# Batched matrix product on one core: groups of four matrices with longer transfer runs, in place of groups of two

## Chip, cores, metric

One core of a Trainium2 chip (trn2) runs the kernel. The time is device microseconds of one execution, given as a median of several runs. The experiments ran on two chips, and each is compared with the kernel before in the same rounds.

## The reference

```python
b1, b2, m, k, n = 8, 16, 256, 512, 384
def reference(x, weight):            # x [8,16,256,512], weight [8,16,512,384], float32
    return np.matmul(x, weight).astype(np.float32)
```

That is 128 independent products. x has 67 MB, weight 101 MB, out 50 MB: 218 MB must cross between HBM (the large memory) and SBUF (the core's own memory; PSUM, below, is where PE leaves its results).

## The kernel before

Five engines run their own programs and meet at semaphores. SP issues all transfers on one queue; DVE casts x and weight to bf16 and copies the transposed x out of PSUM; PE transposes and multiplies; ACT copies the products into the store buffer. G is 2 matrices a group. A partition holds R = 4 consecutive rows of the group, so an x run is 4 x 512 x 4 B = 8 KB, an out run 6 KB, and a weight run (4 rows of one matrix) 6 KB. A *run* is one contiguous piece; each run moves as one transfer packet (the records have packets of 8192 and 6144 B, and one of 4 B for each engine and transfer). The code is cut, and comments in it are added.

```python
    G = 2; C = P // G; R = G * M // P; J = R // G; NG = B // G
    AHEAD = 4
    XS, WS, OS = AHEAD, AHEAD * G, 8          # slots for x, weight, out
    ...
    def load(e, n, n0):
        wait(e, x_cast, n - XS + 1)
        e.dma_start(x_sb[n0 % XS][:],
            x_rows[bass.ds(n * (G * M), G * M)].rearrange("(p r) k -> p r k", r=R),
        ).then_inc(x_in[n0 % XS], 16)
        for i in range(G):                    # one weight transfer a matrix
            wait(e, w_cast, n * G + (i + 1 - WS))
            e.dma_start(w_sb[(n0 * G + i) % WS][:], ...).then_inc(w_in[(n0 * G + i) % WS], 16)
    ...
    @block.sync                               # SP: the order of the queue
    def _(e):
        U = OS
        for n in range(AHEAD):
            load(e, n, n)
        rounds = (NG - AHEAD) // U
        with e.Fori(0, rounds) as t:
            for s in range(U):
                load(e, t * U + (AHEAD + s), AHEAD + s)
                store(e, t * U + s, s)
        for n in range(rounds * U, NG):
            if n + AHEAD < NG:
                load(e, n + AHEAD, n + AHEAD)
            store(e, n, n)
        ...
```

Of the kernel before, what the change touches and what calls it, by code (L numbers as in the profile page):

```python
# [10 lines left out]
@with_exitstack  # L11
def kernel(
    ctx: ExitStack,
    tc: tile.TileContext,
    x: bass.AP,
    weight: bass.AP,
    out: bass.AP,
):
    nc = tc.nc
    P = 128  # L20

    b1, b2, M, K = x.shape
    _, _, _, N = weight.shape
    B = b1 * b2
    KO = K // P

    x_rows = x.rearrange("b1 b2 m k -> (b1 b2 m) k")
    w_rows = weight.rearrange("b1 b2 k n -> (b1 b2 k) n")
    o_rows = out.rearrange("b1 b2 m n -> (b1 b2 m) n")

    fp32 = mybir.dt.float32
    bf16 = mybir.dt.bfloat16



    G = 2
    C = P // G
    R = G * M // P
    J = R // G
    NG = B // G  # L40

    AHEAD = 4

    XS, WS, OS = AHEAD, AHEAD * G, 8
    BS, TS, WBS = 2, 2, 4
    PT, PO = 4, 2

    ctx.enter_context(tc.tile_critical())  # L48

    def sbuf(name, shape, dtype, n):  # L50
        return [
            ctx.enter_context(nc.sbuf_tensor(f"{name}{s}", shape, dtype)) for s in range(n)
        ]

    def psum(name, shape, dtype, n):
        return [
            ctx.enter_context(nc.psum_tensor(f"{name}{s}", shape, dtype)) for s in range(n)
        ]

    def sems(name, n):  # L60
        return [tc.alloc_semaphore(f"{name}{s}") for s in range(n)]


    identity = sbuf("identity", [P, P], fp32, 1)[0]
    x_sb = sbuf("x_sb", [P, R, K], fp32, XS)
    x_bf = sbuf("x_bf", [P, R, K], bf16, BS)


    x_t = sbuf("x_t", [P, J, KO // 2, G, G, C, 2], bf16, TS)
    w_sb = sbuf("w_sb", [P, KO, N], fp32, WS)  # L70
    w_bf = sbuf("w_bf", [P, KO, N], bf16, WBS)
    out_sb = sbuf("out_sb", [P, R, N], fp32, OS)
    pt = psum("pt", [P, 2, KO // 2, P], fp32, PT)
    po = psum("po", [P, J, 512], fp32, PO)




    x_in, w_in, o_out = sems("x_in", XS), sems("w_in", WS), sems("o_out", OS)
    id_done, x_cast, w_cast, t_copied, t_made, p_made, o_copied = (  # L80
        sems(name, 1)[0]
        for name in (
            "id_done", "x_cast", "w_cast", "t_copied", "t_made", "p_made", "o_copied"
        )
    )
    T = R // 2

    def wait(e, sem, value):
        if not isinstance(value, int) or value > 0:
            e.wait_ge(sem, value)  # L90


    def load(e, n, n0):
        wait(e, x_cast, n - XS + 1)
        e.dma_start(  # L95
            x_sb[n0 % XS][:],
            x_rows[bass.ds(n * (G * M), G * M)].rearrange("(p r) k -> p r k", r=R),
        ).then_inc(x_in[n0 % XS], 16)
        for i in range(G):
            wait(e, w_cast, n * G + (i + 1 - WS))  # L100
            e.dma_start(  # L101
                w_sb[(n0 * G + i) % WS][:],
                w_rows[bass.ds(n * (G * K) + i * K, K)].rearrange(
                    "(p ko) n -> p ko n", ko=KO
                ),
            ).then_inc(w_in[(n0 * G + i) % WS], 16)

    def store(e, n, n0):
        e.wait_ge(o_copied, n * G + G)  # L109
        e.dma_start(  # L110
            out=o_rows[bass.ds(n * (G * M), G * M)].rearrange("(p r) n -> p r n", r=R),
            in_=out_sb[n0 % OS][:],
        ).then_inc(o_out[n0 % OS], 16)

    def cast(e, n, n0, t):

        e.wait_ge(x_in[n0 % XS], t * 16)
        wait(e, t_made, n * T + (1 - BS) * T)
        e.tensor_copy(out=x_bf[n0 % BS][:], in_=x_sb[n0 % XS][:]).then_inc(x_cast, 1)  # L119

        def cast_w(i):
            e.wait_ge(w_in[(n0 * G + i) % WS], t * 16)
            wait(e, p_made, n * G + (i + 1 - WBS))
            e.tensor_copy(  # L124
                out=w_bf[(n0 * G + i) % WBS][:], in_=w_sb[(n0 * G + i) % WS][:]
            ).then_inc(w_cast, 1)

        cast_w(0)
        wait(e, p_made, n * G + (1 - TS) * G)
        for q in range(T):  # L130
            e.wait_ge(t_made, n * T + (q + 1))  # L131
            j, g = divmod(2 * q, G)
            e.tensor_copy(  # L133
                out=x_t[n0 % TS][:, j, :, :, g : g + 2].rearrange(
                    "k h i g c e -> k g (h i) (c e)"
                ),
                in_=pt[(n0 * T + q) % PT][:].bitcast(bf16).rearrange(
                    "k g h (i ce) -> k g (h i) ce", i=G
                ),
            ).then_inc(t_copied, 1)  # L140
        for i in range(1, G):
            cast_w(i)

    def multiply(e, n, n0):
        words = x_bf[n0 % BS][:].bitcast(fp32)
        e.wait_ge(x_cast, n + 1)
        for q in range(T):
            wait(e, t_copied, n * T + (q + 1 - PT))
            for rr in range(2):
                for h in range(KO // 2):  # L150
                    ins = e.transpose(  # L151
                        pt[(n0 * T + q) % PT][:, rr, h, :],
                        words[:, 2 * q + rr, h :: KO // 2],
                        identity[:],
                    )
            ins.then_inc(t_made, 1)
        e.wait_ge(t_copied, n * T + T)
        for i in range(G):
            e.wait_ge(w_cast, n * G + (i + 1))
            wait(e, o_copied, n * G + (i + 1 - PO))  # L160
            for j in range(J):
                for ko in range(KO):
                    ins = e.matmul(  # L163
                        po[(n0 * G + i) % PO][:, j, :N],
                        x_t[n0 % TS][:, j, ko // 2, i, :, :, ko % 2].rearrange(
                            "k g c -> k (g c)"
                        ),
                        w_bf[(n0 * G + i) % WBS][:, ko, :],
                        start=(ko == 0),
                        stop=(ko == KO - 1),  # L170
                    )
            ins.then_inc(p_made, 1)

    def copy_out(e, n, n0, t):

        wait(e, o_out[n0 % OS], t * 16)
        for i in range(G):
            e.wait_ge(p_made, n * G + (i + 1))
            for g in range(G):
                ins = e.copy(  # L180
                    out=out_sb[n0 % OS][i * C : (i + 1) * C, g::G, :],
                    in_=po[(n0 * G + i) % PO][g * C : (g + 1) * C, :, :N],
                )
            ins.then_inc(o_copied, 1)

    block = ctx.enter_context(nc.Block())

    @block.gpsimd
    def _(e):
        e.memset(identity[:], 0.0).then_inc(id_done, 1)  # L190
        e.wait_ge(id_done, 1)
        make_identity(nc, identity[:], nomemset=True)
        e.drain().then_inc(id_done, 1)

    @block.sync
    def _(e):
        U = OS
        for n in range(AHEAD):
            load(e, n, n)
        rounds = (NG - AHEAD) // U  # L200
        with e.Fori(0, rounds) as t:  # L201
            for s in range(U):
                load(e, t * U + (AHEAD + s), AHEAD + s)
                store(e, t * U + s, s)
        for n in range(rounds * U, NG):
            if n + AHEAD < NG:
                load(e, n + AHEAD, n + AHEAD)
            store(e, n, n)
        for s in range(OS):
            e.wait_ge(o_out[s], 16 * (NG // OS))  # L210

    @block.vector
    def _(e):
        U = XS
        for n in range(U):
            cast(e, n, n, 1)
        with e.Fori(1, NG // U) as t:
            for s in range(U):
                cast(e, t * U + s, s, t + 1)

    @block.tensor
    def _(e):
        U = 4
        e.wait_ge(id_done, 2)
        for n in range(U):
            multiply(e, n, n)
        with e.Fori(1, NG // U) as t:
            for s in range(U):
                multiply(e, t * U + s, s)

    @block.scalar
    def _(e):
        U = OS
        for n in range(U):
            copy_out(e, n, n, 0)
        with e.Fori(1, NG // U) as t:
            for s in range(U):
                copy_out(e, t * U + s, s, t)


# [28 lines left out]
```

## Time and profile before

| | before |
|---|---|
| median time of the first three runs | 524.96 us |
| the run that was profiled | 526.41 us, span 524.6 us |
| moved, mean rate over the span | 218.16 MB, 416 GB/s |
| busy: PE, DVE, ACT | 65%, 52%, 39% |
| transfer queue | 99.9% |

No compute engine is near full, and the transfer engines are full except at both ends. The prediction below shows and reads the lines. One thing to notice here already: the profiled run was 1.45 us slower than the median that the prediction starts from.

### The profile page before, as it was taken

What the parts mean: (1) busy time and instruction counts of PE and PEld (TensorE: products, weight loads), DVE (VectorE), ACT (ScalarE), POOL (GpSimd) and SP (SyncE); (2) the same over time, 40 slices, a digit from 0 to 9 for tenths busy, and PEclk for the clock granted to TensorE, in tenths of its full rate; (3) what the DMA queues carried; (4) which work ended last, traced back from release to release, by engine and by line L of the source; (5) the groups of instructions that cost most, each with busy time, mean ns of one, the idle gap of its engine ahead of it and who ended that gap; (6) DMA issues with size and microseconds to landing.
All of it is one profiled execution on the core that took longest, in us unless ns stands there. A gap on an engine that the chain in (4) does not pass through costs nothing.

```text
span 524.6 us, 5588 instructions
## 1 busy us (share of the span) xinstructions
PE 338.9 (65%) x1536; PEld 191.9 (37%) x1536; DVE 272.4 (52%) x320; ACT 204.3 (39%) x257; POOL 0.7 (0%) x6
## 2 busy tenths in 40 slices
PE   3755676756747576675776656666657666766764
PEld 2533333333333343343333333333334333433331
DVE  4655454464554554645545446455454464554641
ACT  1652424344333343342433434444334334344242
POOL 0000000000000000000000000000000000000000
PEclk9997868688787877878778778787787878778686
DMA  8999999999999999999999999999999999999995
GB/s 335 421 415 414 422 420 424 424 424 421 424 423 423 424 423 424 425 420 425 423 423 424 420 423 426 421 424 425 422 425 422 424 424 422 424 424 422 426 423 238
DMA packets 36868, 218.16 MB, mean 416 GB/s; under 512 B 4096, under 2 KB 4096, under 8 KB 28672
## 3 DMA queue, kind: packets, MB, share of 16 engines
q1 hardware_dynamic: 36864, 218.12, 99.9%
q14 instruction: 3, 0.02, 0.0%
q8 instruction: 1, 0.02, 0.0%
HBM read 167.77 MB, written 50.33 MB: 416 GB/s over the span
## 4 chain that ended last, share of the span: by engine, by line
SPq 73%; DMA 15%; issue 7%; PE 2%; DVE 1%; ACTq 0%; DVEq 0%; ACT 0%
SPq L101 47%; DMA w_sb<-in_weight_dram 15%; SPq L110 14%; SPq L95 10%; PE po L163 2%; SPq L90 1%; DVE x_t L133 1%; DVE w_bf L124 0%; SPq L109 0%; ACTq _compat.py:109 0%; SPq L201 0%; PE pt L151 0%; DVEq L90 0%; DVEq L131 0%; ACT out_sb L180 0%
## 5 line engine op out<-in xcount | busy, mean ns | idle before, releaser
L180 ACT COPY out_sb<-po 64x768 f32<-64x768 f32 x256 | 203.0, 793 | 314.4 <-PE po L163 311.7
L163 PE MATMUL po<-w_bf,x_t 128*128 128x384 bf16 x1024 | 251.9, 419 | 95.3 <-DVE x_t L133 95.3
L163 PEld LDWEIGHTS po<-w_bf,x_t 128*128 128x128 bf16 x1024 | 119.4, 122 | 216.6 <-issue 182.0
L119 DVE CAST x_bf<-x_sb 128x2048 bf16<-128x2048 f32 x64 | 78.5, 1227 | 200.0 <-DMA x_sb<-in_x_dram 200.0
L124 DVE CAST w_bf<-w_sb 128x1536 bf16<-128x1536 f32 x128 | 122.3, 955 | 40.2 <-DMA w_sb<-in_weight_dram 40.2
L151 PE MATMUL pt<-identity,x_bf 128*128 128x128 f32 x512 | 87.7, 322 | 83.8 <-DVE x_bf L119 83.5
L151 PEld LDWEIGHTS pt<-identity,x_bf 128*128 128x128 f32 x512 | 72.5, 211 | 109.1 <-issue 107.9
L133 DVE COPY x_t<-pt 128x1024 bf16<-128x1024 bf16 x128 | 82.2, 683 | 1.1 <-PE pt L151 1.1
L180 ACT ACT_TABLE_LOAD x1 | 1.3, 1283 | 0.9 <-SPq L48 0.9
masks.py:199 POOL TENSOR_SCALAR_AFFINE_SELECT identity<-identity 128x128 f32<-128x128 f32 x1 | 0.3, 293 | 0.2 <-POOL identity L190 0.2
L190 POOL MEMSET identity<- 128x128 f32 x1 | 0.2, 204 | 0.5 <-SPq L48 0.5
L253 POOL MEMSET const-bfloat16-1.0<- 128x1 bf16 x1 | 0.1, 101 | 0.0
L253 POOL MEMSET const-uint8-127<- 128x1 uint8 x1 | 0.1, 101 | 0.0
L253 POOL MEMSET const-float32-0.0<- 128x1 f32 x1 | 0.1, 98 | 0.2 <-issue 0.2
L253 POOL MEMSET const-float32-1.0<- 128x1 f32 x1 | 0.1, 98 | 0.0
## 6 DMA issues: line engine op xcount, KB each, us to landing
w_sb<-in_weight_dram SPq DMA_DIRECT2D x128, 768.0 KB, 22.3
x_sb<-in_x_dram SPq DMA_DIRECT2D x64, 1024.0 KB, 22.6
out_dram<-out_sb SPq DMA_DIRECT2D x64, 768.0 KB, 21.7
```

The lines of the kernel that those rows point to most:

```text
L90: e.wait_ge(sem, value)
L95: e.dma_start(x_sb[n0 % XS][:], x_rows[bass.ds(n * (G * M), G * M)].rearrange("(p r) k -> p r k", r=R),).then_inc(x_in[n0 % XS], 16)
L101: e.dma_start(w_sb[(n0 * G + i) % WS][:], w_rows[bass.ds(n * (G * K) + i * K, K)].rearrange("(p ko) n -> p ko n", ko=KO),).then_inc(w_in[( ...
L110: e.dma_start(out=o_rows[bass.ds(n * (G * M), G * M)].rearrange("(p r) n -> p r n", r=R), in_=out_sb[n0 % OS][:],).then_inc(o_out[n0 % OS] ...
L119: e.tensor_copy(out=x_bf[n0 % BS][:], in_=x_sb[n0 % XS][:]).then_inc(x_cast, 1)
L124: e.tensor_copy(out=w_bf[(n0 * G + i) % WBS][:], in_=w_sb[(n0 * G + i) % WS][:]).then_inc(w_cast, 1)
L133: e.tensor_copy(out=x_t[n0 % TS][:, j, :, :, g : g + 2].rearrange("k h i g c e -> k g (h i) (c e)"), in_=pt[(n0 * T + q) % PT][:].bitcast( ...
L151: ins = e.transpose(pt[(n0 * T + q) % PT][:, rr, h, :], words[:, 2 * q + rr, h :: KO // 2], identity[:],)
L163: ins = e.matmul(po[(n0 * G + i) % PO][:, j, :N], x_t[n0 % TS][:, j, ko // 2, i, :, :, ko % 2].rearrange("k g c -> k (g c)"), w_bf[(n0 * G ...
L180: ins = e.copy(out=out_sb[n0 % OS][i * C : (i + 1) * C, g::G, :], in_=po[(n0 * G + i) % PO][g * C : (g + 1) * C, :, :N],)
L190: e.memset(identity[:], 0.0).then_inc(id_done, 1)
L253: nc = _bacc.Bacc("TRN2", target_bir_lowering=False, num_devices=1)
```

## The change

The intent is fewer and longer runs: groups of four with 16 KB runs of x and 12 KB runs of out, weight as before. The last four matrices are two pairs, so that the last chain of compute stays short. Stores are issued behind the third later group instead of the fourth, but groups are twice as big. Semaphores start with a bias, so that no special first round is needed.

```diff
-    G = 2
-    R = G * M // P
-    AHEAD = 4
-    XS, WS, OS = AHEAD, AHEAD * G, 8
+    Q = 4
+    QUADS = B // Q - 1
+    PAIRS = [(QUADS, QUADS * Q), (QUADS + 1, QUADS * Q + 2)]
+    J = M // P
+    XS, WS, OS = 2, 8, 4
+    LAG = 3
...
+            x_sb[a.slot(XS)][:, : J * G],
+            x_rows[bass.ds(a.m * M, G * M)].rearrange("(p r) k -> p r k", r=J * G),
...
+            out=o_rows[bass.ds(a.m * M, G * M)].rearrange("(p r) n -> p r n", r=J * G),
+            in_=out_sb[a.slot(OS)][:, : J * G],
...
             for g in range(G):            # now four copies of 32 partitions a matrix
                 ins = e.copy(
-                    out=out_sb[n0 % OS][i * C : (i + 1) * C, g::G, :],
+                    out=out_sb[a.slot(OS)][i * C : (i + 1) * C, g : J * G : G, :],
...
+                load(e, At(t, U, LAG + s))
+                store(e, At(t, U, s))
```

More of the change, by code (lines that the diff above doesn't have):

```diff
@@ L32 @@
     bf16 = mybir.dt.bfloat16
-    G = 2
-    C = P // G
-    R = G * M // P
-    J = R // G
-    NG = B // G
-    AHEAD = 4
-    XS, WS, OS = AHEAD, AHEAD * G, 8
+    Q = 4
+    QUADS = B // Q - 1
+    PAIRS = [(QUADS, QUADS * Q), (QUADS + 1, QUADS * Q + 2)]
+    GROUPS = QUADS + 2
+    J = M // P
+    XS, WS, OS = 2, 8, 4
     BS, TS, WBS = 2, 2, 4
     PT, PO = 4, 2
+    LAG = 3
     ctx.enter_context(tc.tile_critical())
@@ L64 @@
     identity = sbuf("identity", [P, P], fp32, 1)[0]
-    x_sb = sbuf("x_sb", [P, R, K], fp32, XS)
-    x_bf = sbuf("x_bf", [P, R, K], bf16, BS)
-    x_t = sbuf("x_t", [P, J, KO // 2, G, G, C, 2], bf16, TS)
+    x_sb = sbuf("x_sb", [P, J * Q, K], fp32, XS)
+    x_bf = sbuf("x_bf", [P, J * Q, K], bf16, BS)
+    x_t = sbuf("x_t", [P, J * KO // 2 * Q * P * 2], bf16, TS)
     w_sb = sbuf("w_sb", [P, KO, N], fp32, WS)
     w_bf = sbuf("w_bf", [P, KO, N], bf16, WBS)
-    out_sb = sbuf("out_sb", [P, R, N], fp32, OS)
+    out_sb = sbuf("out_sb", [P, J * Q, N], fp32, OS)
     pt = psum("pt", [P, 2, KO // 2, P], fp32, PT)
     po = psum("po", [P, J, 512], fp32, PO)
-    x_in, w_in, o_out = sems("x_in", XS), sems("w_in", WS), sems("o_out", OS)
     id_done, x_cast, w_cast, t_copied, t_made, p_made, o_copied = (
@@ L85, with __init__, slot, turn @@
     )
-    T = R // 2
-    def wait(e, sem, value):
-        if not isinstance(value, int) or value > 0:
-            e.wait_ge(sem, value)
-    def load(e, n, n0):
-        wait(e, x_cast, n - XS + 1)
+    x_in, w_in, o_out = sems("x_in", XS), sems("w_in", WS), sems("o_out", OS)
+    BIAS = 8
+    class At:
+        def __init__(self, t, U, s, G=Q, m=None):
+            self.t, self.U, self.s, self.G = t, U, s, G
+            self.n = t * U + s
+            self.m = self.n * Q if m is None else m
+            self.m0 = s * Q if m is None else m
+            self.old = self.m - (Q if s <= QUADS else 2)
+        def slot(self, S):
+            return self.s % S
+        def turn(self, S):
+            if isinstance(self.t, int):
+                return self.n // S
+            assert self.U % S == 0
+            return self.t * (self.U // S) + self.s // S
+        def w_turn(self, i):
+            if isinstance(self.t, int):
+                return (self.m + i) // WS
+            assert self.U * Q % WS == 0
+            return self.t * (self.U * Q // WS) + (self.s * Q + i) // WS
@@ L95, in load @@
+    def load(e, a):
+        G = a.G
+        if not isinstance(a.n, int) or a.n >= XS:
+            e.wait_ge(x_cast, a.n - XS + 1)
         e.dma_start(
-            x_sb[n0 % XS][:],
-            x_rows[bass.ds(n * (G * M), G * M)].rearrange("(p r) k -> p r k", r=R),
-        ).then_inc(x_in[n0 % XS], 16)
+            x_sb[a.slot(XS)][:, : J * G],
+            x_rows[bass.ds(a.m * M, G * M)].rearrange("(p r) k -> p r k", r=J * G),
+        ).then_inc(x_in[a.slot(XS)], 16)
         for i in range(G):
-            wait(e, w_cast, n * G + (i + 1 - WS))
+            if not isinstance(a.m, int) or a.m + i >= WS:
+                e.wait_ge(w_cast, a.m + (i + 1 - WS))
@@ L101, in load @@
             e.dma_start(
-                w_sb[(n0 * G + i) % WS][:],
-                w_rows[bass.ds(n * (G * K) + i * K, K)].rearrange(
-                    "(p ko) n -> p ko n", ko=KO
-                ),
-            ).then_inc(w_in[(n0 * G + i) % WS], 16)
-    def store(e, n, n0):
-        e.wait_ge(o_copied, n * G + G)
-        e.dma_start(
-            out=o_rows[bass.ds(n * (G * M), G * M)].rearrange("(p r) n -> p r n", r=R),
-            in_=out_sb[n0 % OS][:],
-        ).then_inc(o_out[n0 % OS], 16)
@@ L115, in cast, with store @@
-    def cast(e, n, n0, t):
-        e.wait_ge(x_in[n0 % XS], t * 16)
-        wait(e, t_made, n * T + (1 - BS) * T)
-        e.tensor_copy(out=x_bf[n0 % BS][:], in_=x_sb[n0 % XS][:]).then_inc(x_cast, 1)
+                w_sb[(a.m0 + i) % WS][:],
+                w_rows[bass.ds(a.m * K + i * K, K)].rearrange("(p ko) n -> p ko n", ko=KO),
+            ).then_inc(w_in[(a.m0 + i) % WS], 16)
+    def store(e, a):
+        G = a.G
+        e.wait_ge(o_copied, a.m + (G + BIAS))
+        e.dma_start(
+            out=o_rows[bass.ds(a.m * M, G * M)].rearrange("(p r) n -> p r n", r=J * G),
+            in_=out_sb[a.slot(OS)][:, : J * G],
+        ).then_inc(o_out[a.slot(OS)], 16)
@@ L121, in cast_w, with xt_view, cast @@
+    def xt_view(a):
+        return x_t[a.slot(TS)][:, : J * KO // 2 * a.G * P * 2].rearrange(
+            "k (j h i g c e) -> k j h i g c e", j=J, h=KO // 2, i=a.G, g=a.G, e=2
+        )
+    def cast(e, a):
+        G = a.G
         def cast_w(i):
-            e.wait_ge(w_in[(n0 * G + i) % WS], t * 16)
-            wait(e, p_made, n * G + (i + 1 - WBS))
+            e.wait_ge(w_in[(a.m0 + i) % WS], a.w_turn(i) * 16 + 16)
+            e.wait_ge(p_made, a.m + (i + 1 - WBS + BIAS))
             e.tensor_copy(
-                out=w_bf[(n0 * G + i) % WBS][:], in_=w_sb[(n0 * G + i) % WS][:]
+                out=w_bf[(a.m0 + i) % WBS][:], in_=w_sb[(a.m0 + i) % WS][:]
@@ L126, in cast_w @@
             ).then_inc(w_cast, 1)
+        e.wait_ge(x_in[a.slot(XS)], a.turn(XS) * 16 + 16)
+        e.wait_ge(t_made, a.old + BIAS)
+        e.tensor_copy(
+            out=x_bf[a.slot(BS)][:, : J * G], in_=x_sb[a.slot(XS)][:, : J * G]
+        ).then_inc(x_cast, 1)
         cast_w(0)
-        wait(e, p_made, n * G + (1 - TS) * G)
-        for q in range(T):
-            e.wait_ge(t_made, n * T + (q + 1))
+        e.wait_ge(p_made, a.old + BIAS)
+        xt = xt_view(a)
+        for q in range(G):
+            e.wait_ge(t_made, a.m + (q + 1 + BIAS))
@@ L132, in cast @@
             j, g = divmod(2 * q, G)
             e.tensor_copy(
-                out=x_t[n0 % TS][:, j, :, :, g : g + 2].rearrange(
-                    "k h i g c e -> k g (h i) (c e)"
-                ),
-                in_=pt[(n0 * T + q) % PT][:].bitcast(bf16).rearrange(
+                out=xt[:, j, :, :, g : g + 2].rearrange("k h i g c e -> k g (h i) (c e)"),
+                in_=pt[(a.m0 + q) % PT][:].bitcast(bf16).rearrange(
                     "k g h (i ce) -> k g (h i) ce", i=G
@@ L142, in cast, with multiply @@
             cast_w(i)
-    def multiply(e, n, n0):
-        words = x_bf[n0 % BS][:].bitcast(fp32)
-        e.wait_ge(x_cast, n + 1)
-        for q in range(T):
-            wait(e, t_copied, n * T + (q + 1 - PT))
+    def multiply(e, a):
+        G = a.G
+        words = x_bf[a.slot(BS)][:].bitcast(fp32)
+        e.wait_ge(x_cast, a.n + 1)
+        for q in range(G):
+            e.wait_ge(t_copied, a.m + (q + 1 - PT + BIAS))
             for rr in range(2):
@@ L151, in multiply @@
                     ins = e.transpose(
-                        pt[(n0 * T + q) % PT][:, rr, h, :],
+                        pt[(a.m0 + q) % PT][:, rr, h, :],
                         words[:, 2 * q + rr, h :: KO // 2],
@@ L156, in multiply @@
             ins.then_inc(t_made, 1)
-        e.wait_ge(t_copied, n * T + T)
+        xt = xt_view(a)
+        e.wait_ge(t_copied, a.m + (G + BIAS))
         for i in range(G):
-            e.wait_ge(w_cast, n * G + (i + 1))
-            wait(e, o_copied, n * G + (i + 1 - PO))
+            e.wait_ge(w_cast, a.m + (i + 1))
+            e.wait_ge(o_copied, a.m + (i + 1 - PO + BIAS))
             for j in range(J):
@@ L163, in multiply @@
                     ins = e.matmul(
-                        po[(n0 * G + i) % PO][:, j, :N],
-                        x_t[n0 % TS][:, j, ko // 2, i, :, :, ko % 2].rearrange(
-                            "k g c -> k (g c)"
-                        ),
-                        w_bf[(n0 * G + i) % WBS][:, ko, :],
+                        po[(a.m0 + i) % PO][:, j, :N],
+                        xt[:, j, ko // 2, i, :, :, ko % 2].rearrange("k g c -> k (g c)"),
+                        w_bf[(a.m0 + i) % WBS][:, ko, :],
                         start=(ko == 0),
@@ L172, in multiply, with copy_out, quad, groups @@
             ins.then_inc(p_made, 1)
-    def copy_out(e, n, n0, t):
-        wait(e, o_out[n0 % OS], t * 16)
+    def copy_out(e, a):
+        G = a.G
+        C = P // G
+        e.wait_ge(o_out[a.slot(OS)], a.turn(OS) * 16 + 16)
         for i in range(G):
-            e.wait_ge(p_made, n * G + (i + 1))
+            e.wait_ge(p_made, a.m + (i + 1 + BIAS))
             for g in range(G):
                 ins = e.copy(
-                    out=out_sb[n0 % OS][i * C : (i + 1) * C, g::G, :],
-                    in_=po[(n0 * G + i) % PO][g * C : (g + 1) * C, :, :N],
+                    out=out_sb[a.slot(OS)][i * C : (i + 1) * C, g : J * G : G, :],
+                    in_=po[(a.m0 + i) % PO][g * C : (g + 1) * C, :, :N],
                 )
             ins.then_inc(o_copied, 1)
+    def quad(n):
+        return At(0, 1, n)
+    pairs = [At(0, 1, n, 2, m) for n, m in PAIRS]
+    def groups(e, U, body):
+        with e.Fori(0, QUADS // U) as t:
+            for s in range(U):
+                body(e, At(t, U, s))
+        for n in range(QUADS // U * U, QUADS):
+            body(e, quad(n))
+        for a in pairs:
+            body(e, a)
     block = ctx.enter_context(nc.Block())
@@ L197, in _ @@
         U = OS
-        for n in range(AHEAD):
-            load(e, n, n)
-        rounds = (NG - AHEAD) // U
+        every = [quad(n) for n in range(QUADS)] + pairs
+        for a in every[:LAG]:
+            load(e, a)
+        rounds = (QUADS - LAG) // U
         with e.Fori(0, rounds) as t:
             for s in range(U):
-                load(e, t * U + (AHEAD + s), AHEAD + s)
-                store(e, t * U + s, s)
-        for n in range(rounds * U, NG):
-            if n + AHEAD < NG:
-                load(e, n + AHEAD, n + AHEAD)
-            store(e, n, n)
+                load(e, At(t, U, LAG + s))
+                store(e, At(t, U, s))
+        for n in range(rounds * U, GROUPS):
+            if n + LAG < GROUPS:
+                load(e, every[n + LAG])
+            store(e, every[n])
         for s in range(OS):
-            e.wait_ge(o_out[s], 16 * (NG // OS))
+            e.wait_ge(o_out[s], 16 + 16 * ((GROUPS - s + OS - 1) // OS))
     @block.vector
     def _(e):
-        U = XS
-        for n in range(U):
-            cast(e, n, n, 1)
-        with e.Fori(1, NG // U) as t:
-            for s in range(U):
-                cast(e, t * U + s, s, t + 1)
+        e.sem_inc(t_copied, BIAS)
+        groups(e, 2, cast)
     @block.tensor
     def _(e):
-        U = 4
+        e.sem_inc(t_made, BIAS)
+        e.sem_inc(p_made, BIAS)
         e.wait_ge(id_done, 2)
-        for n in range(U):
-            multiply(e, n, n)
-        with e.Fori(1, NG // U) as t:
-            for s in range(U):
-                multiply(e, t * U + s, s)
+        groups(e, 2, multiply)
     @block.scalar
     def _(e):
-        U = OS
-        for n in range(U):
-            copy_out(e, n, n, 0)
-        with e.Fori(1, NG // U) as t:
-            for s in range(U):
-                copy_out(e, t * U + s, s, t)
+        e.sem_inc(o_copied, BIAS)
+        for s in range(OS):
+            e.sem_inc(o_out[s], 16)
+        groups(e, OS, copy_out)
 _INS = ['x', 'weight']
```

## The prediction

> **What bounds the kernel now.** I read the page first: busy shares, slices, queue, chain, issues.
>
> ```profile
> PE 338.9 (65%) x1536; PEld 191.9 (37%) x1536; DVE 272.4 (52%) x320; ACT 204.3 (39%) x257; POOL 0.7 (0%) x6
> DMA  8999999999999999999999999999999999999995
> GB/s 335 421 415 414 422 420 424 424 424 421 424 423 423 424 423 424 425 420 425 423 423 424 420 423 426 421 424 425 422 425 422 424 424 422 424 424 422 426 423 238
> q1 hardware_dynamic: 36864, 218.12, 99.9%
> SPq 73%; DMA 15%; issue 7%; PE 2%; DVE 1%; ACTq 0%; DVEq 0%; ACT 0%
> w_sb<-in_weight_dram SPq DMA_DIRECT2D x128, 768.0 KB, 22.3
> x_sb<-in_x_dram SPq DMA_DIRECT2D x64, 1024.0 KB, 22.6
> out_dram<-out_sb SPq DMA_DIRECT2D x64, 768.0 KB, 21.7
> ```
>
> No compute engine passes 65%; the transfer engines are full from the second slice to the last but one. The chain blames the queue of SP, but an issue lands 22 us later: at 424 GB/s some 9 MB stand queued, and SP only waits for room. So the bytes set the time (218.1 MB / 524.6 us = 416 GB/s), and only three things can shorten it: cost per transfer packet, the unfilled start, and the unfilled end. I therefore asked for the stretches, and the waits.
>
> ```profile
> 0.00:13.10 13.10, 5.06 (x18) 3.07 (x19) 5.27 (x6) 1.61 (x2) 0.70 (x6) 1.00 0.84 335
> 200.00:300.00 100.00, 66.54 (x292) 37.10 (x290) 52.31 (x61) 39.30 (x51) 0.00 (x0) 0.78 1.02 423
> 511.00:524.60 13.60, 5.93 (x21) 2.82 (x19) 2.74 (x4) 3.17 (x4) 0.00 (x0) 0.63 0.59 246
> ACT out_sb L180 <- PE po L163: 311.7, 92, 10.6
> PE po L163 <- DVE x_t L133: 95.3, 64, 1.7
> ```
>
> The last three numbers of a stretch are granted clock, DMA share and GB/s. The middle is flat at 423 with a DMA share of 1.02; the last 13.6 us move only 246. ACT waits for PE most of the time, so it has room.
>
> From the packet records of the trace I took medians: a packet of 8192 B (x) takes 309 ns, one of 6144 B (weight and out) 234, and the 4 B packet that ends each transfer 9. That is a straight line: (8192 - 6144)/(309 - 234) = 27.3 B/ns, and 309 - 8192/27.3 = 9 ns fixed. But packets overlap slightly (share 1.02), so I also took the distance between the landings of successive transfers. In the start, where only loads run, x takes 2.482 us and weight 1.881. Over the 8 packets of each engine that is 310 and 235 ns: again 27.3 B/ns and 9 to 10 ns fixed. Stores on their own, at the end, take 1.826 us, 228 ns a packet: only 3 ns fixed. Mixed, one old group of two matrices takes 8.05 us.
>
> **The end.** The timeline shows how it is made.
>
> ```profile
> 510.72 0.96 DVE L124 CAST w_bf<-w_sb 128x1536 bf16<-128x1536 f32 x1 [0.60 <-DMA w_sb<-in_weight_dram]
> 513.10 4.91 PE L163 MATMUL po<-w_bf,x_t 128*128 128x384 bf16 x16 [1.09 <-DVE x_t L133]
> 518.05 1.59 ACT L180 COPY out_sb<-po 64x768 f32<-64x768 f32 x2 [0.57 <-PE po L163]
> 519.67 0.33 SPq L110 DMA_DIRECT2D out_dram<-out_sb  x1
> ```
>
> The last weight lands at 510.2 (mean of the 16 engines; the slowest is 2.3 us later), the last store at 522.8: 12.6 us. Four older stores lie behind that weight and take 4 x 1.83 = 7.3 of them, the last store itself 1.83, so some 3.5 us are empty.
>
> **What the Trainium skill says.** "DMA: Bandwidth & Descriptors", Specifications, gives a fabric ceiling of 435 GB/s; the trace's 27.3 B/ns on 16 engines is 437 without the fixed part, and 423 with it, so it agrees. The same page, "Why small descriptors are slow (HBM only)", names a fixed overhead per packet of about 3 cycles; the trace has one, 9 ns for loads. Its iDMA section lists a load stream of 4 KiB rows alone at 408.7 GB/s; my line, 9 + 4096/27.3 = 159 ns, gives 412, so it also holds below the sizes seen here. "Latency and other measured facts" warns of row pitches of 512 KiB and more at powers of two; the runs here stay contiguous and their pitch goes from 8 to 16 KiB. No run yet shows that size.
>
> **The change, part by part.**
>
> *Longer runs.* Four matrices now need one x transfer of 128 runs of 16 KB instead of two of 8 KB, and one store with 12 KB runs instead of two with 6. Weight stays as it was. Per engine and four matrices: x loses 8 packets of 9 ns and one 4 B packet, 0.08 us; out loses 8 packets of 3 ns and one 4 B packet, 0.03. Against that, turning from store to load seems to save a little (2.482 + 2 x 1.881 + 1.826 = 8.07 against 8.05 measured), and half of those turns vanish: +0.02. Sum -0.09 us a group of four, x31 = -2.8 us. Had stores the same 9 ns, and counting every 4 B packet, it would be (16 x 9 + 2 x 9) x 31 = -5.0 us. I take -3.2.
>
> *The end.* The last four matrices are two pairs, so the last compute chain is the old one: 12.6 us from last weight to last landing. But stores now lag three groups: behind the last weight lie two stores of 1.5 MB and one of 0.75, 3 x 1.83 us plus 2 x 1.83 = 9.1 us, where there were 7.3. One store of 0.75 MB moves from ahead of the last load to behind it, into the empty time: up to -1.8 us. The slowest engine, 2.3 us late, has less emptiness than the mean, so I take -1.4.
>
> *Buffers.* x has 2 x 2 MB instead of 4 x 1 MB, weight 8 slots, out 4 x 1.5 instead of 8 x 0.75 MB: the same bytes. A load of x now waits for the cast of the group two before it. When that cast ends, four weights (3 MB), one x group and its weights and a store, about 9 MB, still stand in the queue, some 20 us. So no gap: 0.
>
> *ACT.* Four copies of 32 partitions for each matrix instead of two of 64. A copy's time goes by its 768 elements a partition (793 ns), so 504 copies x 0.793 = 400 us, 77%. The table load is now listed inside the loop: 7 x 1.28 = 9 us more at most. Still under the 16.0 us of a group: 16 x 0.793 = 12.7.
>
> *Other.* The x cast doubles in size and halves in count; PE's work is equal; counters with a bias remove special first rounds and cost well under 1 us.
>
> Sum: 524.96 - 3.2 - 1.4 = **520.4 us**, -0.9%.
>
> **Rivals.** (1) *Compute becomes the bound.* With two PSUM output buffers, the loop of a group of four is: ACT copies two matrices 6.4 us, PE multiplies the last one 2.4, transposes with their copies by DVE about 3.4 (0.6 + 4 x 0.68), PE multiplies the first 2.4: 14.6 us against 16.0 of transfers. If the x_t copies, whose inner runs halve, rose to 1.1 us, it would be 16.3, and the time about 525 + 31 x 0.2 - 1.4 = 530. For it: ACT at 77% and PE's idle before products, 95 us, tied to x_t. Against: the element count and data width are the same. (2) *Long runs gain nothing or lose*, if a 16 KB run is cut into packets of 8 KB or less: then only the end is left, 523.5; if power-of-two starts collide in memory, x slows: 5% of its 159 us (64 x 2.482) is +8, and the time about 531. Against: 8 KB runs show no such loss beside 6 KB ones. (3) *The end gains nothing*, if ACT and PE, behind on the last group of four, delay the pairs: 521.8. I traced it: the last four are copied some 21.5 us after their x lands, the last pair's weights arrive 27 us after it. (4) *All 9 ns per packet are saved, also on stores, and the whole 1.8 at the end*: 518.
>
> **Range and chances.** Transfers -2.5 to -5.0, the end 0 to -1.8, with some room for rival 1: 517.5 to 523.5. Over 2% faster (514.5) would need 8.7 us from the packets besides the whole 1.8 of the end, against 5.0 at the most; slower by 2% (535.5) needs more than rival 1 or 2 makes of it.
>
> **What would show it.** Packets of 16384 B at about 609 ns and of 12288 B at 453 to 459; data packets fewer by 7,900 out of 32,768. x of four landing 4.88 us after its predecessor, a store of four in about 3.65; groups of four every 16.0 us instead of 16.1; middle slices at 426 GB/s. ACT at 77 to 79% with copies still near 793 ns, and x_t copies near 683. From the last weight to the last landing still 12.6 us, with about 1.7 empty. I am wrong if middle slices drop below 423, if DMA slices in the middle fall below 9, or if 16384 B packets are absent.

## The result, and the profile after

Ratios here are the mean time of one kernel's runs over that of the other's of the same rounds, so not quite the ratio of the medians quoted beside them.

The changed kernel took 524.12 us (median of 4; 523.48 to 524.36) against 525.28 for the kernel before: ratio 0.9972, interval 0.995 to 0.9994. It is faster, but by 1.2 to 1.5 us where 4.6 were predicted, and outside the predicted range.

The page of the kernel after: span, busy shares, transfer slices, packets, queue, the group of ACT's copies, ACT's table loads, and the issues with their time to landing.

```profile
span 521.7 us, 5583 instructions
PE 323.8 (62%) x1536; PEld 192.3 (37%) x1536; DVE 270.0 (52%) x289; ACT 406.9 (78%) x511; POOL 0.7 (0%) x6
DMA  8999999999999999999999999999999999999996
GB/s 330 424 422 423 421 427 423 424 423 423 426 431 424 422 421 426 428 429 421 420 427 427 428 424 421 423 427 429 427 422 421 425 429 428 422 423 423 426 427 258
q1 hardware_dynamic: 27936, 218.12, 99.8%
L213 ACT COPY out_sb<-po 32x768 f32<-32x768 f32 (+1 forms) x504 | 397.9, 790 | 107.4 <-PE po L197 100.6
L213 ACT ACT_TABLE_LOAD x7 | 9.0, 1283 | 1.6 <-ACTq L277 1.5
x_sb<-in_x_dram SPq DMA_DIRECT2D x31, 2048.0 KB, 29.6
```

Much of what was predicted is there: ACT at 78% with copies of 790 ns and seven table loads, 27,936 packets instead of 36,864, and a flat transfer row. The packet records show 16384 B packets at 611 ns in the median and 12288 B at 460, within 2 ns of what was worked out. The stretches of 100 us in the middle move 425 and 424 GB/s where they moved 423 and 424:

```profile
200.00:300.00 100.00, 66.18 (x291) 38.63 (x289) 51.05 (x55) 78.48 (x100) 0.00 (x0) 0.73 1.01 425
300.00:400.00 100.00, 61.48 (x296) 36.10 (x296) 50.56 (x54) 82.86 (x105) 0.00 (x0) 0.80 1.01 424
```

The prediction expected 426. The end (timeline; cast of the second last weight, last products, last copies, issue of the last store) has the same length as before, 8.8 us from the first of these lines to the last against 8.95:

```profile
507.13 0.96 DVE L152 CAST w_bf<-w_sb 128x1536 bf16<-128x1536 f32 x1 [0.60 <-DMA w_sb<-in_weight_dram]
509.34 4.95 PE L197 MATMUL po<-w_bf,x_t 128*128 128x384 bf16 x16 [0.97 <-DVE x_t L167]
514.33 1.59 ACT L213 COPY out_sb<-po 64x768 f32<-64x768 f32 x2 [0.56 <-PE po L197]
515.95 0.33 SPq L136 DMA_DIRECT2D out_dram<-out_sb  x1
```

**The place to look is the spread of the 16 engines.** Each transfer raises its semaphore 16 times, and the trace keeps the time of each. I take it as once for each engine: a transfer has 144 packets (36,864 for 256 transfers), 16 times 8 of data and one of 4 B. The kernel waits for all 16, so a transfer counts as landed when the last has come. Sorted for one weight transfer near 480 us of a second trace of the changed kernel, the last engine is 3.6 us behind the median one and the last but one 1.3. In the first trace of before it is 2.3 against 1.0, in its second 2.4 against 1.5. From about 260 us on, in the changed kernel's second trace from 100 us on, the last one falls behind alone, and steadily: behind the median one it is 1.6 and 2.2 us late at 250 us and 2.8 and 3.5 at 450 in the two traces of the changed kernel, 1.4 and 1.55 and then 2.3 and 2.4 before. That it is one and the same engine is likely from this, but the records do not name it.

So I took two speeds for four matrices: the mean of all engines (packet records, between 20 and 200 MB) and the slowest (a straight line through the last landing of each weight, 17th to 120th of 128). The third number is how far the last landing of the last weight is behind the mean of its 16.

| kernel | mean, us | slowest, us | behind at the last weight, us |
|---|---|---|---|
| before, two traces | 16.110, 16.100 | 16.156, 16.135 | 2.30, 2.27 |
| after, two traces | 16.057, 16.064 | 16.093, 16.129 | 2.77, 3.35 |
| both_short | 16.136 | 16.204 | 3.57 |
| store_short | 16.076 | 16.133 | 3.17 |
| short_spread | 16.035 | 16.103 | 3.23 |
| before_batched | 16.131 | 16.238 | 4.27 |
| before_later1 | 16.099 | 16.146 | 2.48 |
| after_lag4 | 16.053 | 16.126 | 3.41 |
| long_spread | 16.021 | 16.097 | 3.25 |
| long_quarters_lag4 | 16.003 | 16.109 | 4.26 |
| act_stores | 16.028 | 16.096 | 2.84 |
| before_act | 16.104 | 16.136 | 3.10 |

Two traces of one kernel agree within 0.01 in the mean but differ by up to 0.036 in the slowest, so a difference of that size in the second column decides nothing. By the means, the change gains about 0.045 us for four matrices, 1.4 us over 31 groups; on the slowest engine 0.035, 1.1 us. The prediction had 0.09 in its sum and then took 0.10.

### The profile page after: what moved, and what is told of

It reads as the page before. It is cut to its first block, busy times and chain, and to the rows that moved or that the text cites. A ratio compares the mean times of both kernels' runs of the same rounds, so it can differ in the third digit from the quotient of the medians.

```text
span 521.7 us, 5583 instructions
## 1 busy us (share of the span) xinstructions
PE 323.8 (62%) x1536; PEld 192.3 (37%) x1536; DVE 270.0 (52%) x289; ACT 406.9 (78%) x511; POOL 0.7 (0%) x6
## 3 DMA queue, kind: packets, MB, share of 16 engines
q1 hardware_dynamic: 27936, 218.12, 99.8%
## 4 chain that ended last, share of the span: by engine, by line
DMA 89%; DVE 7%; issue 1%; PE 1%; SPq 0%; DVEq 0%; ACTq 0%; ACT 0%
DMA x_sb<-in_x_dram 85%; DVE x_bf L158 7%; DMA w_sb<-in_weight_dram 4%; PE po L197 1%; SPq L121 0%; DVE x_t L167 0%; DVE w_bf L152 0%; DVEq L157 0%; ACTq _compat.py:109 0%; ACT out_sb L213 0%; SPq L304 0%; SPq L49 0%
## 5 line engine op out<-in xcount | busy, mean ns | idle before, releaser
L213 ACT COPY out_sb<-po 32x768 f32<-32x768 f32 (+1 forms) x504 | 397.9, 790 | 107.4 <-PE po L197 100.6
L197 PE MATMUL po<-w_bf,x_t 128*128 128x384 bf16 x1024 | 227.6, 380 | 139.9 <-ACT out_sb L213 103.6
L197 PEld LDWEIGHTS po<-w_bf,x_t 128*128 128x128 bf16 x1024 | 104.2, 109 | 254.7 <-ACT out_sb L213 126.9
L158 DVE CAST x_bf<-x_sb 128x4096 bf16<-128x4096 f32 (+1 forms) x33 | 73.6, 2229 | 215.6 <-DMA x_sb<-in_x_dram 215.6
L184 PE MATMUL pt<-identity,x_bf 128*128 128x128 f32 x512 | 96.9, 365 | 50.6 <-DVE x_bf L158 50.6
L152 DVE CAST w_bf<-w_sb 128x1536 bf16<-128x1536 f32 x128 | 117.5, 952 | 1.7 <-DMA w_sb<-in_weight_dram 1.5
L184 PEld LDWEIGHTS pt<-identity,x_bf 128*128 128x128 f32 x512 | 88.1, 218 | 67.0 <-issue 62.3
L167 DVE COPY x_t<-pt 128x1024 bf16<-128x1024 bf16 x128 | 84.4, 687 | 22.9 <-PE pt L184 22.3
```

Of the source, the lines that this page charges most:

```text
L152: e.tensor_copy(out=w_bf[(a.m0 + i) % WBS][:], in_=w_sb[(a.m0 + i) % WS][:]).then_inc(w_cast, 1)
L158: e.tensor_copy(out=x_bf[a.slot(BS)][:, : J * G], in_=x_sb[a.slot(XS)][:, : J * G]).then_inc(x_cast, 1)
L167: e.tensor_copy(out=xt[:, j, :, :, g : g + 2].rearrange("k h i g c e -> k g (h i) (c e)"), in_=pt[(a.m0 + q) % PT][:].bitcast(bf16).rearrange(
L184: ins = e.transpose(pt[(a.m0 + q) % PT][:, rr, h, :], words[:, 2 * q + rr, h :: KO // 2], identity[:],)
L197: ins = e.matmul(po[(a.m0 + i) % PO][:, j, :N], xt[:, j, ko // 2, i, :, :, ko % 2].rearrange("k g c -> k (g c)"), w_bf[(a.m0 + i) % WBS][: ...
L213: ins = e.copy(out=out_sb[a.slot(OS)][i * C : (i + 1) * C, g : J * G : G, :], in_=po[(a.m0 + i) % PO][g * C : (g + 1) * C, :, :N],)
```

## The experiments

Each kernel was timed in five rounds beside the kernel before. All were correct.

| kernel | median, us | before, same chip | ratio | interval |
|---|---|---|---|---|
| before_again | 525.14 | 525.13 | 0.9998 | 0.9982 to 1.0013 |
| after_again | 524.11 | 525.13 | 0.9974 | 0.9961 to 0.9988 |
| both_short | 527.27 | 525.13 | 1.0035 | 1.0021 to 1.0049 |
| store_short | 524.76 | 525.13 | 0.9988 | 0.9974 to 1.0001 |
| before_later1 | 524.89 | 525.48 | 0.9989 | 0.9975 to 1.0002 |
| after_lag4 | 523.92 | 525.48 | 0.9967 | 0.9954 to 0.9981 |
| short_spread | 523.65 | 525.48 | 0.9964 | 0.9950 to 0.9977 |
| before_batched | 528.92 | 525.48 | 1.0066 | 1.0052 to 1.0080 |
| long_spread | 523.42 | 525.85 | 0.9957 | 0.9943 to 0.9971 |
| long_quarters_lag4 | 524.19 | 525.85 | 0.9970 | 0.9956 to 0.9983 |
| act_stores | 523.36 | 525.85 | 0.9956 | 0.9943 to 0.9970 |
| before_act | 526.73 | 525.82 | 1.0015 | 1.0002 to 1.0028 |

### Both kernels once more

No edit.

> The kernel before, unchanged, once more: what it varies by. The four timed runs so far lie at 524.79, 524.96, 525.59 and 526.66 us, and the profiled one, from whose trace the prediction was worked out, at 526.41. Theory A (one distribution): mean near 525.5, spread 1 us or so, the ratio to itself 1.000 within 0.002. Rival (the traced run was a special one): most runs near 524.9 and only a few near 526.5; a trace near 524.9 then shows an emptier loss around the first stores (34 to 48 us) or a smaller lag of the slowest transfer engine at the end.

> The changed kernel, unchanged. Theory A, from the two traces: per group of four the x transfer costs 0.07 us less, the store 0.01 less, turns between load and store 0.02 more, so 0.058 x 31 = 1.8 us; the start costs 0.2 more; the end gains 0.75 because the slowest engine is late. Sum -2.3 us, ratio 0.9955 to 0.996. Rival (the traces flatter it, the compute loop gives something back): ratio 0.9975 or more, and groups of four at 16.1 us or more in the new trace.

Before is one broad distribution (524.36 to 526.22 in these six runs), not a few bad runs among good ones. The change is 0.9974: 1.35 us. The two traces, 524.6 and 521.7 us long, flattered it, since the first was of one of the slower runs (526.41 us). For after_again the rival's ratio came true, but groups of four stayed at 16.06 us, not at 16.1: the compute loop gives nothing back.

### Are the long runs worth what was predicted?

both_short cuts each x transfer and each store of the changed kernel into two of half the run (in the last two pairs too, worth some 0.2 us by 9 and 3 ns a packet). store_short does it for stores alone.

```diff
-        e.dma_start(
-            x_sb[a.slot(XS)][:, : J * G],
-            x_rows[...].rearrange("(p r) k -> p r k", r=J * G),
-        ).then_inc(x_in[a.slot(XS)], 16)
+        for half in range(2):
+            H = J * G // 2
+            e.dma_start(
+                x_sb[a.slot(XS)][:, half * H : (half + 1) * H],
+                x_rows[...].rearrange("(p r) k -> p r k", r=J * G)[:, half * H : (half + 1) * H],
+            ).then_inc(x_in[a.slot(XS)], 16)
         # the same for the store; waits count 32 a turn
```

> The changed kernel with the old run sizes: x in two transfers with 8 KB runs, out in two with 6 KB runs, everything else as changed. Theory A: it loses the 1.8 us of the runs and the 0.2 of the start, and keeps the end's 0.75: 0.5 to 1 us below the kernel before, ratio 0.998 to 0.999; groups of four at 16.10 us. Rival (the compute loop of four gives back what the runs save): slower than the kernel before, ratio above 1.000, with gaps in the transfers of the middle. The prediction's own sizes would put it 3.2 us above the changed kernel.

> The changed kernel with 6 KB runs for out alone, x still in 16 KB runs. Theory A: long store runs earn almost nothing: within 0.4 us of the changed kernel. The prediction's step (0.03 us a group of four) would make it 0.9 us slower, the bigger size it also weighed (9 ns for each of 8 packets, 0.07 us a group) 2.2 us slower.

Undoing both costs 3.2 us against the changed kernel on the same chip (527.27 - 524.11), about 3.0 without the pairs. Undoing the stores alone costs 0.65, so x has some 2.5. By these times the prediction's terms, 0.08 x 31 = 2.5 and 0.03 x 31 = 0.9, about hold. By the means of the table they are smaller: from both_short to the changed kernel 0.072 to 0.079 us a group, 2.2 to 2.4 us. My theory A falls: I had read the store term as nothing from two traces. But both_short is 1.8 us *slower than before* (2.1 by medians) with the same run sizes. Groups of four as such cost time. (Its runs of 8 KB now stand 16 KB apart, a second difference from before, but the packets do not show it: 309 and 234 ns in the median, as before. Its few packets of 4096 B take 159 ns, as the prediction's line has it.) The rival of that run, gaps in the transfers, is not what does it either: in the middle of both_short the transfer engines are as busy as ever (last but one number).

```profile
200.00:300.00 100.00, 60.55 (x299) 35.22 (x297) 51.86 (x56) 80.07 (x101) 0.00 (x0) 0.85 1.02 423
300.00:400.00 100.00, 63.53 (x296) 36.43 (x296) 50.51 (x54) 80.71 (x102) 0.00 (x0) 0.80 1.01 423
```

### The end

before_later1 issues the stores of the kernel before one load group later, as the change does in bytes. after_lag4 sets them one group of four later still.

```diff
-        for n in range(AHEAD):               # before_later1
+        LAG = AHEAD + 1
+        for n in range(LAG):
             load(e, n, n)
-        rounds = (NG - AHEAD) // U
+        rounds = (NG - LAG) // U
...
-    LAG = 3                                  # after_lag4
+    LAG = 4
```

> The kernel before with each store issued one load group later, so that one more store of 0.75 MB lies behind the last weight: the end of the change alone. The prediction read the end from the mean of the 16 transfer engines (3.5 us empty) and would have -1.8 us in full. Theory A (the slowest engine, 2.3 us behind the mean at the last weight, sets the end and has only about 1.1 us empty): -0.7 to -1.1 us, ratio 0.998 to 0.9987, and the last landing of the store before the last lies after the issue of the last store. Rival (the end is fixed by the last compute chain alone): -1.8 us, ratio 0.9965.

> The changed kernel with stores behind the fourth later group instead of the third: 1.5 MB more lies behind the last weight. By the mean of the engines there are still 1.7 us empty at its end, so -1.7 us. Theory A (the slowest engine has nothing empty left): within 0.5 us of the changed kernel, ratio to the kernel before 0.9965 to 0.998.

before_later1 is 0.6 us faster (interval 1.3 faster to 0.1 slower), not 1.8. In its trace the last store is issued at 516.86:

```profile
516.86 0.33 SPq L110 DMA_DIRECT2D out_dram<-out_sb  x1
```

The store just ahead of it lands at 516.82 on the mean engine, but at 519.50 on the slowest, which then has 1.83 us of the last store to do and ends at 521.33. So the mean is empty for over a microsecond while the slowest never rests. after_lag4 shows it again: the mean engine lands the last store at 517.14, 2 us earlier than in the changed kernel's first trace, and the slowest at 520.73, no earlier. Its time is within 0.4 us of the changed kernel's as a ratio to before (0.9967 against 0.9974).

after_lag4 also settles the rival of the compute bound. In its waits ACT stood 61 us for store buffers and PE 162 us for ACT, where the changed kernel has 104 for the latter, and it was no slower:

```profile
PE po L197 <- ACT out_sb L213: 162.2, 79, 6.2
ACT out_sb L213 <- DMA out_dram<-out_sb: 61.0, 20, 3.8
```

### Turns between load and store

What groups of four change, besides run sizes, is how often the queue turns from load to store and back: once for four matrices instead of twice. short_spread puts the turns back into store_short; before_batched takes them out of the kernel before. Compute and transfers are untouched in both.

```diff
-                load(e, At(t, U, LAG + s))   # short_spread, in the loop
-                store(e, At(t, U, s))
+                a = At(t, U, s)              # half a store behind the 2nd and the 4th weight
+                load(e, At(t, U, LAG + s),
+                     lambda i: store(e, a, (i // 2,)) if i % 2 else None)
...
-            for s in range(U):               # before_batched
-                load(e, t * U + (AHEAD + s), AHEAD + s)
-                store(e, t * U + s, s)
+            for s in range(1, U, 2):
+                load(e, t * U + (AHEAD + s), AHEAD + s)
+                load(e, t * U + (AHEAD + s + 1), AHEAD + s + 1)
+                store(e, t * U + s, s)
+                store(e, t * U + (s + 1), s + 1)
```

> As store_short (out in two transfers with 6 KB runs), but in the loop the first half is issued after the second weight of the later group and the second half after the fourth, so that loads and stores alternate as often as in the kernel before; the transfers and the static end are those of store_short. Theory T (a change between load and store saves some time by overlap, and groups of four have half as many): groups of four at 16.04 us or less against 16.08, and 0.8 to 1.2 us faster than store_short, ratio to the kernel before 0.9965 to 0.9975. Rival (the cost of the groups of four lies elsewhere: size of x transfers, compute loop, drift of an engine): within 0.4 us of store_short, 0.998 to 0.9995.

> The kernel before with loads and stores issued two groups at a time (load, load, store, store), the end kept: half as many changes between load and store, run sizes and compute untouched. Theory T: four matrices take 16.13 us instead of 16.10 to 16.11, the whole 0.8 to 1.2 us slower, ratio 1.0015 to 1.0025. Rival: unchanged within 0.4 us, and then it is not the turns.

Both go the way of theory T. short_spread is 1.1 us below store_short by medians, 1.3 by ratios, with 16.035 us against 16.076, which is 1.3 us over 31 groups. The two ran on different chips and the intervals of their ratios just touch, but the kernel before was no faster on short_spread's chip (525.48 against 525.13). The stretches of store_short, then of short_spread:

```profile
200.00:300.00 100.00, 61.55 (x302) 35.93 (x301) 52.13 (x56) 80.42 (x102) 0.00 (x0) 0.83 1.01 425
300.00:400.00 100.00, 66.41 (x296) 39.08 (x296) 50.90 (x54) 80.49 (x101) 0.00 (x0) 0.73 1.01 424
```

```profile
200.00:300.00 100.00, 61.27 (x300) 35.83 (x297) 52.69 (x56) 80.06 (x101) 0.00 (x0) 0.83 1.02 426
300.00:400.00 100.00, 62.73 (x299) 36.56 (x300) 51.20 (x54) 82.69 (x105) 0.00 (x0) 0.79 1.01 425
```

before_batched is 3.5 us slower, three times what I expected, although its mean of 16.131 is just the expected one. Its slowest engine accounts for that: 16.238 against 16.145, which is 0.093 x 31 = 2.9 us, and 4.27 us behind at the last weight, for which the last chain of compute must wait. A price of 0.02 to 0.03 on the mean engine was 0.09 on the one that counts. Why that engine lags more here, the records do not show. Long stretches of one direction are not the whole of it: in short_spread, which has the turns back, it is as late as in store_short (3.23 and 3.17 us), and in the quarters below, which turn most often, 4.26.

### Can both be had?

long_spread keeps 12 KB runs and cuts each store by partitions (every second one) instead of by rows; long_quarters_lag4 cuts it in four, behind each weight, with the stores a group later; act_stores issues the stores of the loop from ACT's queue, so that both directions share the engines: in its trace, whenever store packets of that queue are in flight, they are 7.9 on average beside 8.2 packets of loads, and a store lands 11.9 us after its issue.

```diff
+        for part in parts:                   # long_spread: 2 parts; quarters: 4
+            p = slice(part, 128, 2)
+            e.dma_start(out=o_rows[...].rearrange(...)[p],
+                        in_=out_sb[a.slot(OS)][p, : J * G]).then_inc(o_out[a.slot(OS)], 16)
...
+        def copy_and_store(e, a):            # act_stores, on ACT; SP keeps the last five groups' stores
+            copy_out(e, a)
+            if not isinstance(a.n, int) or a.n < QUADS - LAG:
+                store(e, a)
```

> The changed kernel with each store of a group of four cut into two transfers of every second partition, 12 KB runs kept, placed after the second and the fourth weight of the later group: the turns of the kernel before together with the long runs of the change. Theory T: what short_spread gained (1.1 us) plus what long store runs are worth (0.65 us by store_short): 523.0 us, ratio 0.995, groups of four at 16.02 us. Rival (store runs and turns are the same gain, not two): as short_spread, 0.9964.

> As long_spread, but in four transfers of every fourth partition, one after each weight, and stores behind the fourth later group (worth 0.2 to 0.4 us by after_lag4): twice the turns of the kernel before. Theory T: below long_spread by another 0.7 to 1.3 us, ratio 0.993 to 0.9935, groups of four at 16.0 us or less. Rival (no more to be had from turns than the kernel before has): within 0.4 us of long_spread.

> The changed kernel with the stores of the first 28 groups issued by ACT on its own queue right behind their copies, so that loads and stores share the engines packet by packet; the end stays on SP as it is. Theory T carried to its limit: groups of four at 16.0 us or less, 1 us or more faster than the changed kernel, if ACT (78% busy) is not held up by issuing. Rival (mixing itself earns nothing, only short bursts on one queue do; or a held-up ACT slows the copies): no faster than the changed kernel, ratio 0.9974 or more.

long_spread (0.9957) and act_stores (0.9956) have the lowest ratios measured, 2.2 to 2.3 us below before. Both lie below the changed kernel's 0.9974, but the intervals overlap, so that they beat it is likely, not shown. Whether long_spread beats short_spread (0.9964) is open for the same reason. The quarters have the best mean of all, 16.003, and are no better than the changed kernel: their slowest engine is 4.26 us behind at the last weight.

before_act does for the kernel before what act_stores did for the changed one: stores 0 to 55 from ACT's queue.

```diff
             for s in range(U):               # SP
                 load(e, t * U + (AHEAD + s), AHEAD + s)
-                store(e, t * U + s, s)
...
             for s in range(U):               # ACT
                 copy_out(e, t * U + s, s, t)
+                store(e, t * U + s, s)
```

> The kernel before with its first 56 stores issued by ACT on its own queue behind their copies, the last 8 on SP as they were: loads and stores mix packet by packet, run sizes, groups and compute untouched. What act_stores did for groups of four (median engine 16.03 to 16.01 us for four matrices, slowest engine 16.11 to 16.10; 0.8 us in the time) it should do here by about the same: 16.07 and 16.12 against 16.095 and 16.145, so -0.6 to -1.0 us, ratio 0.998 to 0.999. Rival (alternating every 8 us already gives all that mixing can give): within 0.3 us, ratio 0.9995 to 1.0005.

I was wrong: it is slower, 1.0015. The row of rates falls to 397 in the second slice (420 in before_again, shown second), but that is made up soon: 20 MB are through at 50.7 us (50.8 and 50.5 in the traces of before), 200 MB at 476.0 (476.1 and 475.6). What differs is the slowest engine, 3.1 us behind at the last weight instead of 2.3. Its lag does not grow steadily here but swings, between 1.6 and 5.0 us behind the median engine after 50 us, so the straight line of the table, 16.136, is no speed in this run.

```profile
GB/s 339 397 425 424 423 420 425 425 422 423 426 421 426 421 424 425 422 423 425 423 423 425 423 424 424 423 426 421 424 424 422 425 423 422 424 423 419 425 424 227
```

```profile
GB/s 336 420 418 420 423 425 421 422 424 421 424 424 423 423 423 423 425 421 425 424 422 425 422 423 425 421 425 424 423 426 422 424 424 423 425 423 424 424 423 254
```

So mixing on two queues is no gain by itself, and why it costs here is open.

## Why the prediction was wrong

**The bound: right.** Transfers set the time, and nothing on PE, DVE or ACT replaced them, though ACT doubled its work (after_lag4).

The step that failed is the sum for the transfers, -2.8 us, taken as -3.2. The next three paragraphs are its parts.

**Longer runs: right in kind, too large.** Predicted 2.5 us for x and 0.9 for out. By times, both_short and store_short give about 2.5 and 0.65. But part of that is the slowest engine, and on the mean engine less is saved. In the start of the changed kernel an x of four lands 4.90 us after its predecessor, where two old ones take 2 x 2.482: 0.07 a group, not 0.08. At its end a store of four takes 3.65, where two old ones take 2 x 1.83: 0.01, not 0.03. (The prediction's own sign, "a store of four in about 3.65", already was no less than two old stores.) Together that is 2.5 us instead of 3.4, and the means of both_short and the changed kernel agree (2.2 to 2.4).

**The turns: this term failed.** The prediction put "half of those turns vanish" at +0.02 us a group, 0.6 in all. Where the order alone was changed, it was more: 1.1 to 1.3 us in groups of four (short_spread against store_short), 3.5 in the kernel before (before_batched). On the mean engine it is 0.03 to 0.04 a group, about 1 us. The price came from the difference of two sums of 8 us (8.07 and 8.05), read on the mean engine; in before_batched the slowest engine lost three times as much.

**The slowest engine: left out of the middle.** It was taken off at the end alone. At the last weight it is 2.3 us behind before, and 2.8 and 3.4 in the changed kernel (3.6 in both_short): about 0.8 us lost, for which the sum had no term. All kernels with groups of four have 2.8 us or more, with turns put back or not, so the turns alone do not explain it; its cause stays open.

**The end: half.** Predicted -1.4; alone it gives -0.6 (before_later1; the interval includes no gain at all). The prediction named the slowest engine, 2.3 us late, and took off only 0.4 for it. Its own numbers would have given more: of the 3.5 us empty on the mean engine, only 3.5 - 2.3 = 1.2 were empty there. In the trace of before that engine lands the store before the last at 520.0 and the last at 522.9, of which 1.8 is work: 1.1. Nor did 12.6 us from the last weight to the last landing hold: on the mean engine the changed kernel has 13.0 and 13.9, since its last compute waits for the later slowest engine.

**Buffers: 0, right.** No slice of the middle falls below 9 tenths of DMA in any trace.

**Rounding.** The steps summed to -2.8 for the packets and -3.2 was taken, without a reason that a run bears out.

Put together in measured terms: -2.5 for the runs, +1.0 for the turns, +0.8 for the slowest engine and -0.6 for the end make -1.3. Measured is -1.35, with an interval from -0.6 to -2.0. Each term is uncertain by some tenths, so that the sum fits so well is luck in part. The transfers alone are -0.7 in this sum, and -1.1 by the slopes of the slowest engine, where -3.2 was taken.

## What to carry to other kernels

When a queue of transfers is the bound, work out the gain on the slowest of the 16 engines, not on their mean: a transfer has landed, and the kernel has ended, only with the last one. A longer run pays its fixed cost per packet once, and the kind of gain can be predicted from packet records. Its size is a difference of a few ns in several hundred, so leave it room: here it was 2.5 us instead of 3.4. And check what the larger group does to the order of loads and stores, for halving the turns took back a third or more of the gain here. If both are wanted, cut the stores and put the pieces between the loads (long_spread; likely better than the change, not shown).

## What the Trainium skill lacked or had wrong

- "DMA: Bandwidth & Descriptors", "Why small descriptors are slow (HBM only)", speaks of a fixed cost per packet for small descriptors. It still counts at 8 KB: 9 to 10 ns a load packet, and going to 16 and 12 KB was worth 3 us of 527 (2.2 to 2.4 by the mean engine).
- The same page gives, for trn2, no cost for stores apart from loads. Alone, a store of 768 KB took 1.826 us and a load of the same size 1.881.
- No page I read tells what turning between loads and stores is worth on one queue. Halving the turns cost 3.5 us of 525 (before_batched), and putting them back in groups of four gained 1.1 to 1.3 (short_spread).
- The iDMA section of that page says in passing that a bulk load runs at the pace of its slowest engine. Here it decides the end of a kernel with loads and stores on one queue: the last engine lost 0.45 us in 100 us before and about 0.6 after (250 to 450 us), and was 2.3 to 4.3 us behind at the last weight.
